# mLSTM heads of a hybrid layer: a head's first values and keys begun in the third chunk of the head in front, its second pair's in its own first chunk

## The chip, the cores and the metric

The kernel runs on one core of one Trainium2 chip. The metric is device time in microseconds (us) of one execution. An execution has a span, from the first to the last instruction that the profile shows, and a little time around it. Before the change three timed runs gave 1699.35, 1700.01 and 1708.68 us, median 1700.01.

## The reference, cut to what matters

One decoder layer over 2048 tokens of width 1024, batch 1, all in float32. An RMS norm, one input projection, two groups of heads beside each other, one output projection, a residual and a last norm:

```
u = rms_norm(x, norm_g)
q_g, k_g, v_g, z_g, r_g, x_m, z_m = split(u @ w_in)
o_g = gla(q_g, k_g, v_g, log_sigmoid(r_g @ up + b) / 16)       # 4 heads, key 128, value 256
c   = silu(causal_conv4(x_m) + conv_b)                          # 1024 wide
q_m, k_m, v_m = c @ blockdiag(w_q), c @ blockdiag(w_k), x_m @ blockdiag(w_v)
i, f = gates of [q_m, k_m, v_m]
h_m = mlstm(q_m, k_m, v_m, i, f)                                # 4 heads of 256
o_m = (rms_norm(h_m) * g + skip * c) * silu(z_m)
out = rms_norm(x + [rms_norm(o_g) * g * silu(z_g), o_m] @ w_out)
```

The mLSTM part is a recurrence per head with a matrix state C and a vector state n: C = f C + i v kT, n = f n + i k, and h = C q / max(|n q|, 1), with exponential input gates and a running maximum that keeps them in range. It may be done chunk by chunk: inside a chunk by a masked 'attention' matrix, between chunks by the state. Only this part of the kernel is touched.

## The kernel before, in words

**Stages.** The tokens are cut into 4 blocks of 512, a block into 4 chunks of 128. TensorE (PE) goes through the input projections of the mLSTM group for the 4 blocks, then through those of the GLA group for the 4 blocks, then through the output projection. A float32 product of full accuracy is made of three fp32r matmuls on a high and a low part (`mm3`, line 193; three matmuls with 512 columns are one *step* of the projection below). One projected tile of 128 x 512 is 8 steps (24 matmuls, tile `pp`); a block of the mLSTM group has 16 of them: X0 to X7 (`xm_drain`, the first two taken as a pair, 16 steps) and Z0 to Z7 (`zm_drain`, the last two as a pair).

**The heads.** Between the steps of the projection PE does the heads, `mattn(b, h)` from line 810. A head forms `pqp` (queries, line 818), then `pma` (line 831, the chunk-by-chunk attention matrices), which `asplit` (line 784) takes out of PSUM: a copy on ScalarE (ACT) and a subtraction on VectorE (DVE), then a mask on GpSimd (POOL). `prep_v(p)` (line 842) forms the values of chunk pair p: 4 matmuls into `pmv`, two copies on ACT and two fused operations on DVE that make `v1` and `v1l`, and two small DVE copies. `prep_c(p)` (line 860) forms the keys: 4 transposes into `pmc`, one copy on ACT (`ctk`, line 869), one subtraction on DVE (`ctl`, line 870). `prep_q(c)` (line 875) splits the queries of chunk c into `qx` with one copy on ACT and one subtraction on POOL; it does nothing for chunk 0 of block 0. None of the three starts a DMA or uses SyncE.

Then come the 4 chunks (line 891). A chunk needs `C`, a scaled copy of the state in two parts (lines 898 and 899, two buffers, so both are in use until the chunk before is through with them); `pmu` (line 904), the state's update, 6 matmuls that read `v1` and `ctk`, `ctl`; `pmo` (line 912), the output, 3 matmuls on the attention matrix and 6 on `qx` and `C`; and the norm of the output (lines 918 to 931: `dn`, `r`, `jk`, `rs`, `on`). Chunks 0 and 1 read pair 0, chunks 2 and 3 pair 1. At the end `fin_pair` (line 795, twice) transposes the outputs (`pt`) and multiplies in the gains and the gate; `spill` sends them to memory. `v1`, `v1l`, `ctk`, `ctl` have two buffers each, one a pair. All of `pqp`, `pma`, `pmv`, `pmc` and `pt` share the two PSUM slots of the pool `ps_t`.

**What sets the order.** PE's order is written out by hand, by a planner: class `Order`, line 104. Projection and heads are generators. The planner keeps a clock `od.t` that each planned matmul advances by a nominal length; a generator that yields a number is due again that much later, one that yields a name waits until the name is in `od.done`. Of those due, the oldest head goes first, then the younger one, then the projection (line 129); the projection yields after every step. Two heads are active at a time (line 126): the third is begun when the first is done. The two PSUM slots are planned for by `od.wait()` and `od.hold(drain)`: after a use, the slot counts as free `drain` us of planned time later; after `pma` that is `od.hold(0.00)` (line 833). The other engines' order is found by a scheduler from priorities; `ahead(tc, n)` and `at(tc, n)` move instructions n places forward. Each engine then works its list off in that order, and real waits are semaphores.

**Around the change.** A head that has its attention matrix waits for the name `mm` of the head in front (line 881), set when that head's chunk 3 is issued (line 942). Then it does

```
        yield from od.wait()
        prep_q(0)
        prep_v(0)
        od.hold(1.80)
        yield from od.wait()
        prep_c(0)
        od.hold(1.10)
        yield 2.10
```

and its chunks. Behind chunk 0 it issues `prep_v(1)`, behind chunk 1 `prep_c(1)` (line 938), each with `od.hold(2.10)`, and between chunks it yields 0.20 and 1.90.

Of the kernel before, what the change touches and what calls it, by code (L numbers as in the profile page):

```python
# [25 lines left out]
H = 4  # L26
# [60 lines left out]
@contextmanager  # L87
def ahead(tc, n):

    tc.cur_priority -= n  # L90
    yield
    tc.cur_priority += n


def at(tc, n):
    def wrap(f):
        def g(*a):
            with ahead(tc, n):
                return f(*a)
        return g  # L100
    return wrap
# [58 lines left out]
def fast_path(ctx, tc, inside, xT, x, w_fm, w_v, w_r, wqT, wkT, wvT, wv, wg, w_up, b_g,  # L160
              norm_g, gla_g, conv_w, conv_b, b_if, ml_g, skip, w_out, fin_g, out):
    nc = tc.nc
    od = Order(tc)
# [24 lines left out]
    def mm(o, l, r, start, stop, **k):  # L188
        n = o.free_size()
        od.t += max(n, 256) / 2400.0 if l.dtype == F32R else max(4 * n, 64) / 2400.0  # L190
        nc.tensor.matmul(o, l, r, start=start, stop=stop, **k)  # L191
# [618 lines left out]
    def mattn(b, h):  # L810
        yield f"x{b}"
        yield 4.00
        qp = gq.tile([P, 2, TB], F32, name="qp", tag="qp", bufs=3)
        ost = gp.tile([P, 2, TB], F32, name="ost", bufs=2)
        for e in range(2):
            t = 2 * h + e
            yield from od.wait()
            pq = ps_t.tile([P, TB], F32, name="pqp", tag="pt")
            mm(pq, wqk[:, t, :], cm[t], True, True)
            with ahead(tc, HPP):  # L820
                nc.scalar.copy(qp[:, e, :], pq)
            with ahead(tc, HPO):
                nc.scalar.activation(ost[:, e, :], cm[t], AF.Copy, scale=skp[:, t:t + 1])
            od.hold(2.40)
            yield 0
        yield from od.wait()
        pa = ps_t.tile([P, TB], F32, name="pma", tag="pt")
        for c in range(NC):
            cs = slice(c * P, (c + 1) * P)
            for e in range(2):  # L830
                mm(pa[:, cs], cm[2 * h + e][:, cs], qp[:, e, cs], e == 0, e == 1)
        A = asplit(pa)
        od.hold(0.00)
        yield f"gr{b}"
        wk, wkh, wkl, ga, fl = gts[b]
        if h not in Tm:
            Tm[h] = gp.tile([P, 2, 258], F32, name=f"Tm{h}", tag=f"T{h}")
        T = Tm[h]
        kv = {}

        @at(tc, HPV)
        def prep_v(p):
            pv = ps_t.tile([P, 2, 2, P], F32, name="pmv", tag="pt")
            v1 = gp.tile([P, 2, 258], F32R, name="v1", tag="v1", bufs=2)
            v1l = gp.tile([P, 2, 258], F32R, name="v1l", tag="v1l", bufs=2)
            for i in range(2):
                c = 2 * p + i
                for e in range(2):
                    mm(pv[:, i, e, :], xm[2 * h + e][0][:, 4 + c * P:4 + (c + 1) * P], wvs[:, 2 * h + e, :], True, True)
            for i in range(2):  # L850
                w1 = wk[:, 2 * p + i, h:h + 1]
                p1 = pv[:, i].rearrange("p e t -> p (e t)")
                nc.scalar.activation(v1[:, i, 0:DV], p1, AF.Copy, scale=w1)
                nc.vector.scalar_tensor_tensor(v1l[:, i, 0:DV], p1, w1, v1[:, i, 0:DV].bitcast(F32), op0=ALU.mult, op1=ALU.subtract)
                kv[2 * p + i] = [(v1[:, i, :], v1l[:, i, :]), None]
            for x_, w_ in ((v1, wkh), (v1l, wkl)):
                nc.vector.tensor_copy(x_[:, :, DV:DV + 2], w_[:, 2 * p:2 * p + 2, h:h + 1].bitcast(F32).broadcast_to([P, 2, 2]))

        @at(tc, HPV)
        def prep_c(p):  # L860
            pv = ps_t.tile([P, 2, 2, P], F32, name="pmc", tag="pt")
            ctk = gp.tile([P, 2, 2, P], F32R, name="ctk", tag="ctk", bufs=2)
            ctl = gp.tile([P, 2, 2, P], F32R, name="ctl", tag="ctl", bufs=2)
            for i in range(2):
                c = 2 * p + i
                for e in range(2):
                    tr(pv[:, i, e, :], cm[2 * h + e][:, c * P:(c + 1) * P])
                kv[c][1] = (ctk[:, i], ctl[:, i])
            nc.scalar.copy(ctk, pv)
            nc.vector.tensor_tensor(ctl, pv, ctk.bitcast(F32), op=ALU.subtract)  # L870

        qx = {}

        @at(tc, HPQ)
        def prep_q(c):
            if c < NC and (b or c):
                qx[c] = gp.tile([P, 2, 2, P], F32R, name="qx", tag="ca", bufs=2)
                split(qx[c][:, 0], qx[c][:, 1], qp[:, :, c * P:(c + 1) * P], QX)

        if (b, h) != (0, 0):  # L880
            yield f"mm{b}_{h - 1}" if h else f"mm{b - 1}_{H - 1}"
        yield from od.wait()
        prep_q(0)
        prep_v(0)
        od.hold(1.80)
        yield from od.wait()
        prep_c(0)
        od.hold(1.10)
        yield 2.10
        on = {}  # L890
        for c in range(NC):
            cs = slice(c * P, (c + 1) * P)
            first = b == 0 and c == 0
            last = b == NB - 1 and c == NC - 1
            if not first:
                Ch, Cl = (gp.tile([P, 2, 258], F32R, name="C", tag="C", bufs=2) for i in range(2))
                with ahead(tc, HPX):
                    nc.scalar.activation(Ch, T, AF.Copy, scale=ga[:, c, h:h + 1])
                    nc.vector.scalar_tensor_tensor(Cl, T, ga[:, c, h:h + 1], Ch.bitcast(F32), op0=ALU.mult, op1=ALU.subtract)
            v1, ctk = kv[c]  # L900
            if not last:
                for e in range(2):
                    pu = ps_u.tile([P, 258], F32, name="pmu", tag="pu")
                    mm3(pu, (ctk[0][:, e, :], ctk[1][:, e, :]), v1, True, True)
                    with ahead(tc, HPT):
                        if first:
                            nc.scalar.copy(T[:, e, :], pu)
                        else:
                            nc.vector.scalar_tensor_tensor(T[:, e, :], T[:, e, :], ga[:, c, h:h + 1], pu, op0=ALU.mult, op1=ALU.add)
                yield 0  # L910
            po = ps_o.tile([P, 258], F32, name="pmo", tag="po")
            mm3(po, (A[:, c, :], A[:, NC + c, :]), v1, True, first)
            if not first:
                for e in range(2):
                    mm3(po, (qx[c][:, 0, e, :], qx[c][:, 1, e, :]), (Ch[:, e, :], Cl[:, e, :]), False, e == 1)
            prep_q(c + 1)
            with ahead(tc, HPN):
                r = sp.tile([P, 1], F32, name="r", bufs=4)
                dn = sp.tile([P, 1], F32, name="dn")
                nc.vector.tensor_scalar(dn, po[:, DV:DV + 1], -1.0, fl[:, c, h:h + 1], op0=ALU.mult, op1=ALU.max)  # L920
                nc.vector.tensor_tensor(r, dn, po[:, DV:DV + 1], op=ALU.max)
                nc.vector.reciprocal(r, r)
                jk = sp.tile([P, DV], BF16, name="jk", bufs=1)
                ss = sp.tile([P, 1], F32, name="ss", bufs=4)
                nc.scalar.activation(jk, po[:, 0:DV], AF.Square, scale=r, accum_out=ss)
                rs = sp.tile([P, 1], F32, name="rs", bufs=4)
                rsqrt(rs, ss, DV)
                nc.vector.tensor_tensor(rs, rs, r, op=ALU.mult)
                o = gp.tile([P, DV], F32, name="on", bufs=4)
                if MON:  # L930
                    nc.scalar.activation(o, po[:, 0:DV], AF.Copy, scale=rs)
                else:
                    nc.vector.tensor_scalar(o, po[:, 0:DV], rs, None, op0=ALU.mult)
            on[c] = o
            yield 0.20
            if c < 2:
                yield from od.wait()
                (prep_v, prep_c)[c](1)
                od.hold(2.10)
            if c < NC - 1:  # L940
                yield 1.90
        od.done.add(f"mm{b}_{h}")
        if f"z{b}_{h}" not in od.done:
            yield f"z{b}_{h}"
        yield from od.wait()
        fin_pair([on[0], on[1]], zsm[b, h], mlg[:, 2 * h:2 * h + 2], 0, ost, True)
        od.hold(1.80)
        yield 3.50
        yield from od.wait()
        fin_pair([on[2], on[3]], zsm[b, h], mlg[:, 2 * h:2 * h + 2], 2 * P, ost, True)  # L950
        od.hold(2.80)
        spill(b, KT + 2 * h, ost)
        od.done.add(f"m{b}_{h}")
# [823 lines left out]
```

## Time and profile before

| | before |
|---|---|
| timed runs (us) | 1699.35, 1700.01, 1708.68; median 1700.01 |
| the profiled execution (us) | 1708.55 |
| its span (us) | 1706.3 |
| PE busy in the span | 1621.9 us (95%) |
| DVE, ACT, POOL busy | 56%, 41%, 26% |
| mean granted TensorE clock | 0.982 of full speed |
| stage: mLSTM heads | about 111 to 702 us |

The busy time of PE is the sum of its matmuls as the profile models them, so 95% says that PE is hardly ever without a matmul in flight; what is left is idle time, and a view of the waits names what ended each piece of it. A line of the timeline gives the start, the length, the engine, the line of the kernel, the operation, output <- inputs, the shapes and the count of the merged instructions; in square brackets the idle time of that engine just before and what ended it. Matmuls overlap, so their length is more than their share of the time; the distance of two starts is what one costs. The granted clock is 1.00 at 2.4 GHz and 0.50 at 1.2 GHz; a stretch's figure is the mean.

### The profile page before, as it was taken

Reading aid. Unit: us, or ns where it says so; the run is one execution under the profiler, and the core shown is the slowest. Engines: PE = TensorE matmul, PEld = TensorE weight load, DVE = VectorE, ACT = ScalarE, POOL = GpSimd, SP = SyncE. Lnnn points to the kernel's source line nnn. Section 1 sums busy time; section 2 is a strip of 40 time slices with the busy share of each in tenths; the row PEclk is TensorE's granted clock in tenths of the full one; section 3 lists DMA queues with packets and bytes.
Section 4 is the critical chain, followed back from the end, with each engine's and each line's share of the span. In section 5 each row is a group of like instructions: output and inputs, shape, how many; then the busy total and the mean of one; then the engine's idle time right before and its main releaser. Section 6 shows DMA issues by size and latency. Waiting matters only on the chain.

```text
span 1706.3 us, 25559 instructions
## 1 busy us (share of the span) xinstructions
PE 1621.9 (95%) x8840; PEld 1362.2 (80%) x8840; DVE 954.7 (56%) x2125; ACT 695.3 (41%) x1486; POOL 444.4 (26%) x422
## 2 busy tenths in 40 slices
PE   7989899999999999899999999999999999999997
PEld 5768777887888788789888888888888877887776
DVE  4956775775667577734442334233513556567663
ACT  4656754564455455412232223122313433243331
POOL 3433421220121024344303120302031304223330
PEclk9999999999999999999999999999999999999999
DMA  7577667636564766576858685758575565574441
GB/s 269 198 261 240 227 218 233 193 111 212 196 196 149 228 195 201 195 251 218 311 168 305 201 283 190 253 173 285 193 252 199 168 237 200 166 247 136 162 145 67
DMA packets 221258, 355.42 MB, mean 208 GB/s; under 512 B 24368, under 2 KB 58160, under 8 KB 221120
## 3 DMA queue, kind: packets, MB, share of 16 engines
q1 hardware_dynamic: 221120, 353.70, 62.5%
q8 instruction: 72, 1.18, 0.3%
q14 instruction: 66, 0.54, 0.1%
HBM read 253.86 MB, written 102.89 MB: 209 GB/s over the span
## 4 chain that ended last, share of the span: by engine, by line
PE 45%; DMA 5%; DVE 4%; issue 2%; POOL 2%; ACT 2%; SPq 0%; POOLq 0%; DVEq 0%; ACTq 0%
PE py L191 16%; PE pp L191 15%; PE pv L191 9%; PE po L191 2%; DMA wlo<-w_dr 1%; DMA whi<-w_dr 1%; DVE bc L1078 1%; PE pu L191 1%; POOL ring L1213 1%; PE pt L201 1%; PE pa L191 1%; DMA f<-q_dr 1%; DMA ring<-in_w_out 0%; PE ptk L201 0%; DMA o1l<-o_dr 0%
## 5 line engine op out<-in xcount | busy, mean ns | idle before, releaser
L191 PE MATMUL pp<-uh,whi 128*128 128x512 f32 x1008 | 421.5, 418 | 11.9 <-ACT whi L214 6.0
L191 PE MATMUL pp<-ul,whi 128*128 128x512 f32 x1008 | 400.1, 397 | 0.5 <-DVE ul L404 0.4
L191 PE MATMUL pp<-uh,wlo 128*128 128x512 f32 x1008 | 400.3, 397 | 0.0
L191 PEld LDWEIGHTS pp<-uh,whi 128*128 128x128 f32 x1008 | 192.0, 190 | 52.6 <-ACT whi L214 7.1
L191 PEld LDWEIGHTS pp<-uh,wlo 128*128 128x128 f32 x1008 | 191.4, 190 | 47.4 <-DMA wlo<-w_dr 1.1
L191 PEld LDWEIGHTS pp<-ul,whi 128*128 128x128 f32 x1008 | 192.0, 190 | 39.9 <-issue 4.8
L215 POOL TENSOR_TENSOR wlo<-wraw,whi 128x512 fp32r<-128x512 f32 (+1 forms) x97 | 133.5, 1382 | 159.2 <-ACT whi L214 56.7
L1213 POOL TENSOR_TENSOR ring<-ring,ring 128x512 f32<-128x512 f32 x77 | 106.1, 1383 | 247.0 <-DMA ring<-in_w_out 117.2
L191 PE MATMUL pv<-whi,uh 128*128 128x256 f32 (+1 forms) x512 | 151.5, 296 | 15.5 <-DVE zs L581 8.8
L191 PE MATMUL pv<-wlo,uh 128*128 128x256 f32 (+1 forms) x512 | 148.5, 290 | 0.5 <-DMA wlo<-w_dr 0.5
L191 PE MATMUL pv<-whi,ul 128*128 128x256 f32 (+1 forms) x512 | 148.4, 290 | 0.0
L191 PE MATMUL py<-f,as 128*128 128x512 f32 x540 | 135.0, 402 | 9.4 <-DVE yf L1308 4.2
L214 ACT CAST as<-ring 128x512 fp32r<-128x512 f32 x105 | 65.0, 621 | 169.3 <-PE py L191 118.1
L191 PEld LDWEIGHTS py<-f,as 128*128 128x128 f32 x540 | 103.6, 193 | 35.2 <-ACT f L214 9.3
L215 POOL TENSOR_TENSOR qx<-qp,qx 128x256 fp32r<-128x256 f32 x60 | 55.7, 932 | 274.8 <-ACT qx L214 274.8
L191 PEld LDWEIGHTS pv<-whi,uh 128*128 128x128 f32 x512 | 100.1, 196 | 18.0 <-DVE zs L581 9.6
L191 PEld LDWEIGHTS pv<-wlo,uh 128*128 128x128 f32 x512 | 99.9, 195 | 1.6 <-DMA wlo<-w_dr 1.6
L191 PEld LDWEIGHTS pv<-whi,ul 128*128 128x128 f32 x512 | 100.1, 195 | 0.7
L215 DVE TENSOR_TENSOR as<-ring,as 128x512 fp32r<-128x512 f32 x105 | 84.8, 811 | 12.2 <-ACT as L214 11.4
L645 DVE SCALAR_TENSOR_TENSOR c<-xm,cw,c 128x512 f32<-128x512 f32 x96 | 78.2, 822 | 14.2 <-ACT c L643 13.4
L221 POOL TENSOR_TENSOR grs<-rsa,nhalf 128x2 f32<-128x2 f32 x32 | 23.6, 738 | 198.4 <-DVE rsa L220 187.7
L985 DVE TENSOR_TENSOR vl<-pv,v 128x256 fp32r<-128x256 f32 x56 | 23.5, 422 | 89.3 <-ACT v L983 89.3
(341 smaller groups left out, 3156.5 us busy)
## 6 DMA issues: line engine op xcount, KB each, us to landing
whi<-w_dr SPq DMA_DIRECT2D x212, 256.0 KB, 3.8
wlo<-w_dr SPq DMA_DIRECT2D x212, 256.0 KB, 4.2
wraw<-in_w_fm SPq DMA_DIRECT2D x80, 256.0 KB, 3.9
w_dr<-whi SPq DMA_DIRECT2D x76, 256.0 KB, 3.4
w_dr<-wlo SPq DMA_DIRECT2D x76, 256.0 KB, 3.4
o_dr<-ost SPq DMA_DIRECT2D x64, 256.0 KB, 3.5
ring<-o_dr SPq DMA_DIRECT2D x60, 256.0 KB, 3.1
ul<-u_dr SPq DMA_DIRECT2D x56, 256.0 KB, 4.6
```

Source lines behind the costliest of these rows:

```text
L191: nc.tensor.matmul(o, l, r, start=start, stop=stop, **k)
L201: nc.tensor.transpose(o, i, ident)
L214: nc.scalar.copy(hi, raw)
L215: (nc.gpsimd if "l" in pool else nc.vector).tensor_tensor(lo, raw, hi.bitcast(F32), op=ALU.subtract)
L221: nc.gpsimd.tensor_tensor(dst, a, nhalf.broadcast_to(list(src.shape)), op=ALU.pow)
L645: nc.vector.scalar_tensor_tensor(ca, xt[:, 1 + j:1 + j + TB], cw[:, t, j:j + 1], ca, op0=ALU.mult, op1=ALU.add)
L985: nc.vector.tensor_tensor(vl[b, h][t // 2][:, t % 2, :], pv[:, :DV], vv[b, h][:, t, :].bitcast(F32), op=ALU.subtract)
L1078: nc.vector.tensor_tensor_scan(w3[:, c], ones, w3[:, c], 0.0, op0=ALU.mult, op1=ALU.add)
L1213: nc.gpsimd.tensor_tensor(o, a, b, op=ALU.subtract)
```

## The change

The wait on the head in front is cut in two. The new name `mp` is set in chunk 2 of a head, after its 0.20. The next head waits for it, and then does `prep_v(0)`, `prep_c(0)` and its 2.10; only then it waits for `mm`, if that isn't set yet, and does `prep_q(0)`, which stood ahead of `prep_v(0)`. The second pair's two preparations both stand behind chunk 0, each with its own wait and hold, and nothing behind chunk 1.

```diff
+        before = f"{b}_{h - 1}" if h else f"{b - 1}_{H - 1}"
         if (b, h) != (0, 0):
-            yield f"mm{b}_{h - 1}" if h else f"mm{b - 1}_{H - 1}"
+            yield "mp" + before
         yield from od.wait()
-        prep_q(0)
         prep_v(0)
         od.hold(1.80)
         yield from od.wait()
         prep_c(0)
         od.hold(1.10)
         yield 2.10
+        if (b, h) != (0, 0) and "mm" + before not in od.done:
+            yield "mm" + before
+        prep_q(0)
         on = {}
         for c in range(NC):
...
             yield 0.20
-            if c < 2:
-                yield from od.wait()
-                (prep_v, prep_c)[c](1)
-                od.hold(2.10)
+            if c == 0:
+                for prep in (prep_v, prep_c):
+                    yield from od.wait()
+                    prep(1)
+                    od.hold(2.10)
+                    yield 0
+            if c == 2:
+                od.done.add(f"mp{b}_{h}")
             if c < NC - 1:
                 yield 1.90
```

## Rows read from the trace of the kernel before

**Rows 1.** The page's first part: busy time of each engine, share of the span, instructions.

```profile
PE 1621.9 (95%) x8840; PEld 1362.2 (80%) x8840; DVE 954.7 (56%) x2125; ACT 695.3 (41%) x1486; POOL 444.4 (26%) x422
```

**Rows 2.** PE's waits between 100 and 700 us: who waited for whom; us in total, times, longest.

```profile
PE pmu L191 <- DVE ctl L870: 9.7, 14, 1.2
PE pmu L191 <- ACT ctk L869: 8.8, 7, 2.9
PE pt L201 <- DVE v1l L854: 4.5, 4, 1.8
```

**Rows 3.** The timeline at chunk 2 of head 0 of block 0: PE's `pmc` of the second pair, ACT's work, and PE's next `pmu`.

```profile
123.03 0.60 PE L201 MATMUL pmc<-ident,c 128*128 128x128 f32 x4
...
127.55 0.47 ACT L925 ACTIVATE jk<-pmo,r 128x256 bf16<-128x256 f32 x1 [1.00 <-DVE r L922]
...
128.01 0.58 ACT L869 CAST ctk<-pmc 128x512 fp32r<-128x512 f32 x1
...
128.64 0.58 PE L191 MATMUL pmu<-v,ctk 128*128 128x258 f32 x1 [2.92 <-ACT ctk L869]
...
129.78 0.58 PE L191 MATMUL pmu<-v,ctl 128*128 128x258 f32 x1 [0.35 <-DVE ctl L870]
```

**Rows 4.** Four stretches of the span: stretch, length, busy time of PE, PEld, DVE, ACT, POOL with their instructions, mean granted clock, DMA share, GB/s. Below them starts of the projection's matmuls at either level of the clock.

```profile
126.00:136.00 10.00, 7.02 (x25) 6.05 (x26) 7.07 (x19) 4.83 (x13) 4.46 (x6) 0.66 0.77 262
208.00:218.00 10.00, 6.83 (x30) 5.28 (x29) 9.32 (x29) 7.86 (x17) 4.17 (x5) 0.83 0.46 152
290.00:300.00 10.00, 7.89 (x46) 6.49 (x45) 7.59 (x24) 6.14 (x16) 2.69 (x4) 1.00 0.51 161
453.00:461.00 8.00, 6.12 (x26) 5.23 (x26) 4.80 (x17) 3.63 (x10) 1.97 (x3) 0.79 0.41 132
...
133.59 0.63 PE L191 MATMUL pp<-uh,wlo 128*128 128x512 f32 x1
134.02 0.63 PE L191 MATMUL pp<-uh,whi 128*128 128x512 f32 x1
...
135.14 0.40 PE L191 MATMUL pp<-uh,whi 128*128 128x512 f32 x1
135.37 0.40 PE L191 MATMUL pp<-ul,whi 128*128 128x512 f32 x1
```

**Rows 5.** PE's timeline from the end of head 1 to chunk 0 of head 2 in block 1, and the first `pqp` of head 3.

```profile
327.21 0.88 PE L191 MATMUL pmo<-C,qx 128*128 128x258 f32 x6
327.93 0.39 PE L191 MATMUL pp<-uh,whi 128*128 128x512 f32 x1
...
328.62 0.60 PE L201 MATMUL pt<-ident,on 128*128 128x128 f32 x4
329.06 1.06 PE L191 MATMUL pmv<-wvs,xm 128*128 128x128 f32 x8
329.87 0.48 PE L191 MATMUL pp<-uh,whi 128*128 128x512 f32 x1
...
331.35 0.60 PE L201 MATMUL pmc<-ident,c 128*128 128x128 f32 x4
...
333.18 0.60 PE L201 MATMUL pt<-ident,on 128*128 128x128 f32 x4
...
334.32 0.28 PE L191 MATMUL pmu<-v,ctk 128*128 128x258 f32 x1
...
336.82 1.06 PE L191 MATMUL pmv<-wvs,xm 128*128 128x128 f32 x8
...
338.40 1.02 PE L191 MATMUL pqp<-c,wqk 128*128 128x512 f32 x2
```

**Rows 6.** How `pma`'s slot is drained: PE, ACT and DVE behind chunk 2 of head 2 in block 0, and ACT and DVE where no chunk stands ahead (block 1, before the heads).

```profile
184.18 1.95 PE L191 MATMUL pma<-qp,c 128*128 128x128 f32 x16
185.89 0.48 PE L191 MATMUL pp<-uh,whi 128*128 128x512 f32 x1
...
187.10 0.48 ACT L931 ACTIVATE on<-pmo,rs 128x256 f32<-128x256 f32 x1 [1.36 <-DVE rs L928]
187.47 0.58 ACT L788 CAST A<-pma 128x512 fp32r<-128x512 f32 x1
...
188.09 0.69 DVE L789 TENSOR_TENSOR A<-pma,A 128x512 fp32r<-128x512 f32 x1 [1.02 <-ACT A L788]
...
268.66 0.59 ACT L788 CAST A<-pma 128x512 fp32r<-128x512 f32 x1 [2.44 <-PE pma L191]
...
269.34 0.68 DVE L789 TENSOR_TENSOR A<-pma,A 128x512 fp32r<-128x512 f32 x1
```

**Rows 7.** ACT, DVE and POOL right behind chunk 3 of head 1 in block 1: `C` and `qx` of head 2's chunk 0.

```profile
328.01 0.73 ACT L898 ACTIVATE C<-Tm,ga 128x516 fp32r<-128x516 f32 x1 [1.87 <-PE pmo L191]
328.65 0.39 ACT L214 CAST qx<-qp 128x256 fp32r<-128x256 f32 x1
...
328.78 0.76 DVE L899 SCALAR_TENSOR_TENSOR C<-Tm,ga,C 128x516 fp32r<-128x516 f32 x1
...
329.12 1.00 POOL L215 TENSOR_TENSOR qx<-qp,qx 128x256 fp32r<-128x256 f32 x1 [1.07 <-ACT qx L214]
```

**Rows 8.** How `pmv`'s slot is drained: a second pair's `pmv` and its last DVE operation (block 1, head 1).

```profile
312.12 1.05 PE L191 MATMUL pmv<-wvs,xm 128*128 128x128 f32 x8
...
315.71 0.48 DVE L854 SCALAR_TENSOR_TENSOR v1l<-pmv,wk,v 128x256 fp32r<-128x256 f32 x1 [0.93 <-ACT v L853]
```

## The prediction, made before the change was built

> **What bounds the kernel now.** Read the page's first part first: PE has a matmul in flight for 1621.9 us, 95% of the span, while DVE has 56% and ACT 41% [rows 1]. The change adds no work to any engine. It can only take idle time from PE, give it new idle time, or change the clock at which PE works. So the next view is PE's waits in the heads' stage [rows 2]: 9.7 + 8.8 = 18.5 us in 21 waits of `pmu` for `ctl` and `ctk`, and 4.5 us in 4 waits of a `pt` for the slot of a `pmv`. All 21 lie at a chunk 2, the first reader of the second pair. The timeline at the worst shows why [rows 3]: `pmc` was issued at 123.03, but its copy stands in ACT's list behind `jk`, which waited for the norm's `r`; `ctk` began at 128.01, and PE stood still for 2.92 us, then 0.35 more for `ctl`. Last, the clock behind such waits [rows 4]: behind three of them it is granted at half (1.2 GHz) for a while. A mean of 0.66 over 10 us is 6.8 us at half, 0.83 over 10 us is 3.4, 0.79 over 8 us is 3.4: 13.6 us. At half a projection matmul costs 134.02 - 133.59 = 0.43 us, at full 0.23, so 13.6 x (1 - 0.23/0.43) = 6.3 us are lost there. (The fourth stretch holds such waits too, PE idle for 2.1 us of 10, and stayed at 1.00.)
>
> The Trainium skill (TensorE: Matmul & The Clock Gate, section Terms) prices throttled time at that time x (1 - K/N); at half this makes 13.6 x 0.5 = 6.8 us, an estimate; the trace has 6.3, and the sum takes the trace's.
>
> **The change part by part.** Times are those of the profiled execution, 1708.55 us (span 1706.3 and 2.25 around it), which is 8.5 us above the median of 1700.01; the difference worked out on the one is carried to the other.
>
> *(a) The second pair's keys, a chunk earlier.* Now `pmc` has three steps of the projection, chunk 1 and four steps between itself and chunk 2: 3 x 0.70 + 1.8 + 4 x 0.70 = 6.7 us (a step is 3 x 0.23; in a chunk 6 matmuls take 327.93 - 327.21 = 0.72 [rows 5], 0.12 each, and it has 15). The slowest case of before took from the end of `pmc` (123.63) to the second wait's end (129.78) 6.1 us [rows 3]. So the 21 waits go: -18.5, and with them the three stretches at half clock: -6.3. If the cover were too short, each us missing would come back at its chunk 2. What is late next is the slots of PSUM, (c) and (d).
>
> *(b) `prep_q(0)` behind the wait.* It is passed by `prep_v(0)` and `prep_c(0)`: its ACT copy stands behind three more ACT copies, its POOL subtraction behind none. Chunk 0 now may follow chunk 3 of the head in front at once, with one step, `pt`, `pmu` and 3 matmuls of `pmo` between: 0.70 + 0.44 (329.06 - 328.62) + 0.72 + 0.36, less the 0.16 by which the next matmul begins before the modelled end: some 2.1 us from the end of the last `pmo`. What is needed just there can be seen [rows 5, 7]: that `pmo` ends at 327.21 + 0.88 = 328.09; `C` begins on ACT at 328.01 and is whole on DVE at 329.54, `qx` on POOL at 330.12, 1.45 and 2.03 us after. Both just fit, because the scheduler puts early what is ready early. Bounds: nothing gained, since no wait for `qx` is in the trace; lost at most the 1.4 us of a `qx` from start to end (328.65 to 330.12), at 6 places (two heads in each of blocks 1 to 3): 0 to 8 us. I take 0, the row that is at that very place.
>
> *(c) The first pair, begun at `mp`.* Here the order must be followed through the planner, whose nominal lengths fix only the order (a step 0.64, a chunk 1.61, `prep_v` 0.85, `prep_c` 0.43, `fin_pair` 0.43, `pqp` 0.85, `pma` 1.71). I did this by hand; for the kernel before it gives exactly the sequence of rows 5. Put 0 at a block's first `prep_v(0)`. Head 0 does chunk 0 at 3.8, then `prep_v(1)` and `prep_c(1)`, chunk 1 at 9.3, chunk 2 at 13.5, `mp` at 15.7. Head 1, ready since before the heads, prepares its first pair 15.7 to 17.0; chunk 3 of head 0 at 17.6, its first `fin_pair` at 19.9, chunk 0 of head 1 at 20.3, 1.1 us behind that chunk in place of the 334.32 - 328.09 = 6.2 us of rows 5. But head 2 is begun only when head 0 is done (25.8), pays its 4.00, and has `pqp` at 32.0 and 32.8. Then chunk 3 of head 1 (35.0), `pma` of head 2 (36.6), `fin_pair` of head 1 (38.3) and `prep_v(0)` of head 2 (38.7) follow each other without a step between. Head 3, begun at 43.0, has chunk 2 of head 2 (53.7), its `pma` (55.3), its `prep_v(0)` (57.0) and `prep_c(0)` (57.8), again without a step. So twice in each block a preparation needs the slot that `pma` holds, and the planner lets it, for `od.hold(0.00)` says that slot is free at once. Before, chunk 3 and three steps stood there.
>
> What the slot takes: `pma` ends at 186.13, ACT's copy begins at 187.47 behind `on`, DVE is through at 188.78, 2.65 us after the end; where no chunk stands ahead, 268.66 + 1.36 [rows 6]. The next matmul may begin 0.24 before that end (185.89). Head 2: `pt` takes 0.44, `prep_v(0)` waits 2.65 + 0.24 - 0.44 = 2.4 us. Head 3: `prep_v(0)` takes 0.81 (329.06 to 329.87 [rows 5]), `prep_c(0)` waits 2.1 us. All of PE's list waits behind it, the chunks and the projection too. 4 blocks x 4.5 = +18 us. With the short drain it is 4 x (1.15 + 0.85) = 8 us. I take 18, since a chunk with its `on` stands ahead both times, as in the long row; the ends stay 8 and 18.
>
> These would be even gaps that recur at one place of every block. The Trainium skill (Perfetto Trace Analysis, section Optimization Strategy) says that consistent bubbles can mean that PSUM has no room for the next tile; it has no price for it, and the gaps of before aren't of this kind, as they wait for `ctk` and `ctl` to be written.
>
> *(d) The last `fin_pair` behind `prep_v(1)`.* For heads 0 and 2 its `pt` now takes the slot of the next head's second `pmv`, with `pmc` and three steps between: 0.44 (as `pt`, 4 transposes) + 3 x 0.70 - 0.24 = 2.3 us after its end. A second pair's `pmv` ended at 313.17 and was drained at 316.19, 3.0 us after [rows 8]: 0.7 us of wait, 8 times, +5.6. In exchange the 4 waits of rows 2 go, -4.5: together +1.1. Bounds: -4.5 if nothing waits, and 8 x 1.8 - 4.5 = +9.9 if each is as long as the longest of rows 2.
>
> *(e) The clock behind the new waits.* Of the waits of before, the 2.92 us was followed by 6.8 us at half, others by 3.4 us, and those of the fourth stretch by none [rows 3, 4]. I let three of the eight of (c) have 3.4 us at half, 3.4 x 0.465 = 1.6 each: +4.7. Bounds 0 and 8 x 3.2 = 25 (6.8 us each).
>
> Sum: -18.5 - 6.3 + 0 + 18 + 1.1 + 4.7 = -1.0 us: 1707.5 for the profiled execution, 1699 against the median. The GLA and output stages keep their work and, but for a small shift at their start, their order: 0.
>
> **The rivals.** *All gain:* the slots are free in time. ACT's order is made anew, and if `A`'s copy no longer stands behind `on`, the drain is 1.36 us: -18.5 - 6.3 + 8 and (d) at 0, no clock lost: -17, 1683 us. For it: no wait for `pma`'s slot is among rows 2, and 1.36 us has occurred [rows 6]. Against: the same two instructions would stand there in the same distance.
>
> *Slower:* one mechanism, the eight waits of (c) take the clock with them. Its place is each `pmv` or `pmc` right behind a `pma`. The other terms make -23.7, so it breaks even at 3.0 us a place and is over 0.5% slower from (23.7 + 8.5)/8 = 4.0. A wait of 2.25 with 3.4 us at half makes 3.85; with half of them at 6.8 us 4.65, or +37 in all: +13.5, 1713 us. For it: three of the waits of before did so. Against: the fourth stretch of rows 4, as much idle, didn't.
>
> *It doesn't do what it says:* my planner's walk is wrong and a third wait for the name `mp` or a drain brings the preparations back to where they were; then (a) is given back in part and nothing else changes: about -5 to 0, 1697.
>
> **How the numbers follow.** Within 0.5% (8.5 us, about what a measurement of this kernel can tell from no change) lie the forecast and the third rival. Forecast 0.43, all gain 0.31, slower 0.21, the third 0.05. A small part of the forecast's own range (1690 to 1708) is beyond 0.5%: faster 0.33, same 0.45, slower 0.22. The range goes from the all-gain case to the slower one: 1682 to 1713.
>
> **What would show it.** (a) is right if no `pmu` waits for `ctk` or `ctl` any more. (c) is right if PE's waits list `pmv` and `pmc` for DVE `A` of line 789, four each, of 2.4 and 2.1 us; wrong, if they are under 1 us or the two names don't occur. (b) is wrong if `pmo` waits for `qx` or `C`. (d) shows as `pt` waiting for `v1l`, eight times instead of four. (e) shows in the granted clock behind the waits of (c). Behind chunk 3 of heads 0 and 2 the next head's chunk 0 should begin after some 1.1 us, behind that of head 1 as late as now or later. The prediction falls with (c): without those waits the kernel is 1% faster.

## The result, and the profile after

The changed kernel takes 1722.9 us (median of 4 runs), the kernel before 1701.7 (median of 4, three of them those of the table above): the ratio is 1.012, 95% interval 1.0101 to 1.014. Forecast were 1699 us, range 1682 to 1713: it is slower, and outside the range. The profiled execution after is 1721.2 us with a span of 1719.4; that of before lay 7 us above its own median, so the two profiles differ by 12.7 us only. For the heads' stage there is a better mark in the same two traces: the first `pa`, with which the heads of the GLA group begin, starts at 747.1 us before and at 765.6 after, 18.5 later. Its row in each:

```profile
747.14 0.38 PE L191 MATMUL pa<-qt,kt 128*128 128x128 f32 x2
...
765.60 0.38 PE L191 MATMUL pa<-qt,kt 128*128 128x128 f32 x2
```

The page's first part shows the same work as [rows 1]:

```profile
PE 1625.9 (95%) x8840; PEld 1367.8 (80%) x8840; DVE 958.7 (56%) x2125; ACT 693.4 (40%) x1486; POOL 439.7 (26%) x422
```

PE's waits of the changed kernel from 100 to 710 us (us in total, times, longest); they answer to [rows 2]. The lines of a chunk have numbers 3 higher than before, those behind `mattn` 7 higher.

```profile
PE pmv L191 <- DVE A L789: 12.4, 4, 4.0
PE pmc L201 <- DVE A L789: 11.1, 4, 3.7
PE pt L201 <- DVE ctl L870: 7.2, 10, 1.0
PE pt L201 <- ACT on L934: 3.1, 1, 3.1
PE pmu L191 <- DVE Tm L912: 1.4, 4, 0.6
PE pt L201 <- DVE v1l L854: 1.3, 1, 1.3
...
PE pmu L191 <- DVE ctl L870: 0.8, 1, 0.8
```

Only two of these rows wait for data that they read, `pt` for `on` and `pmu` for `ctl`. `pmv` doesn't read `A`, `pmc` doesn't read `A`, `pt` doesn't read `ctl`: each waits for a slot of PSUM whose last reader is the instruction named, and so do `pmu` for `Tm` and `pt` for `v1l`. That is how a slot wait looks in this view. The 18.5 us for `ctk` and `ctl` have gone down to 0.8; 23.5 us for the slot that `pma` held have come, and `pt` waits 11.6 in place of 4.5.

The timeline of block 3, from `pma` of head 2 to the `pmv` behind it (the counterpart of [rows 6]):

```profile
650.13 1.95 PE L191 MATMUL pma<-qp,c 128*128 128x128 f32 x16
...
651.50 1.77 POOL L215 TENSOR_TENSOR wlo<-wraw,whi 128x512 fp32r<-128x512 f32 x1
...
652.15 0.15 DVE L220 TENSOR_SCALAR rsa<-ss 128x1 f32<-128x1 f32 x1
653.24 0.72 POOL L215 TENSOR_TENSOR qx<-qp,qx 128x256 fp32r<-128x256 f32 x1
...
653.92 0.54 POOL L221 TENSOR_TENSOR rs<-rsa,nhalf 128x1 f32<-128x1 f32 x1
...
654.50 0.16 DVE L931 TENSOR_TENSOR rs<-rs,r 128x1 f32<-128x1 f32 x1 [2.19 <-POOL rs L221]
...
654.69 0.47 ACT L934 ACTIVATE on<-pmo,rs 128x256 f32<-128x256 f32 x1 [2.57 <-DVE rs L931]
655.06 0.58 ACT L788 CAST A<-pma 128x512 fp32r<-128x512 f32 x1
655.67 0.69 DVE L789 TENSOR_TENSOR A<-pma,A 128x512 fp32r<-128x512 f32 x1 [0.62 <-ACT A L788]
...
656.51 0.68 PE L191 MATMUL pmv<-wvs,xm 128*128 128x128 f32 x4 [3.99 <-DVE A L789]
```

Read it from the bottom. PE stood still for 3.99 us ahead of `pmv`. The slot came free with DVE's subtraction; that had ACT's copy of `A` ahead of it, which stood behind `on`; `on` waited for `rs`, and `rs` for POOL, for which `rsa` was ready at 652.30, but which did a piece of the projection's weights (`wlo`) and a `qx` first. So a drain of two instructions, 0.58 + 0.69 = 1.3 us, lasted 4.3 us from the end of `pma` (652.08) to that of `A` (656.36).

In the table, for each kernel's profile: PE's waits from 100 to 710 us added up over the view's rows, the parts of them that matter, and the time at half clock in that stretch, added up from the trace's clock records. Each ratio is to the kernel before, timed beside it. The stretch is the same time in all, not the same work: in kernels 7, 10 and 11 it takes in a wait of 2.8 us of the GLA group (`pv` for `zs`) that ends behind 710 us in the others.

| kernel | ratio to before | all waits | `pmv`, `pmc` for `A` | `pmu` for `ctk`, `ctl` | `pt` | half clock |
|---|---|---|---|---|---|---|
| before | 1 | 26.4 | 0 | 18.5 | 4.5 | 13.7 |
| changed | 1.012 | 39.9 | 23.5 | 0.8 | 11.6 | 27.3 |
| 1: changed, hold 2.40 | 0.9963 | 25.1 | 0.7 | 1.9 | 10.0 | 17.1 |
| 2: second pair's half alone | 0.9951 | 20.9 | 0 | 0.3 | 7.2 | 13.7 |
| 3: first pair's half alone | 1.0036 | 30.6 | 0 | 13.9 | 6.6 | 10.2 |
| 4: before, hold 2.40 | 1.0006 | 31.3 | 0 | 19.1 | 8.1 | 13.7 |
| 5: changed, norm later | one run | 47.1 | 23.3 | 0.6 | 20.1 | 44.4 |
| 6: changed, queries first | 1.011 | 40.2 | 22.4 | 1.9 | 11.9 | 13.7 |
| 7: as 2, hold 2.80 | 0.9916 | 22.4 | 0 | 0 | 4.9 | 13.7 |
| 8: as 1, holds 3.10 | 0.9962 | 24.2 | 1.2 | 0.3 | 7.4 | 10.2 |
| 9: changed, no power | one run | 20.1 | 14.4 | 0 | 1.6 | 13.8 |
| 10: before, no power | 0.9912 | 18.8 | 0 | 11.1 | 1.3 | 6.8 |
| 11: as 9, timed | 0.9915 | 24.4 | 16.8 | 0.8 | 1.7 | 6.8 |

### The profile page after: what moved, and what is told of

Read it like the earlier page. It is cut to its first block, busy times and chain, and to the rows that moved or that the text cites. A ratio compares the mean times of both kernels' runs of the same rounds, so it can differ in the third digit from the quotient of the medians.

```text
span 1719.4 us, 25574 instructions
## 1 busy us (share of the span) xinstructions
PE 1625.9 (95%) x8840; PEld 1367.8 (80%) x8840; DVE 958.7 (56%) x2125; ACT 693.4 (40%) x1486; POOL 439.7 (26%) x422
## 4 chain that ended last, share of the span: by engine, by line
PE 70%; DVE 11%; DMA 6%; issue 4%; POOL 4%; ACT 4%; SPq 1%; POOLq 0%; ACTq 0%; DVEq 0%
PE pp L191 32%; PE py L191 14%; PE pv L191 10%; PE po L191 2%; PE pmo L191 2%; PE pqp L191 1%; PE pmu L191 1%; POOL rs L221 1%; PE pt L201 1%; DVE bc L1085 1%; DVE C L902 1%; PE pu L191 1%; POOL wlo L215 1%; PE pma L191 1%; DMA whi<-w_dr 1%
## 5 line engine op out<-in xcount | busy, mean ns | idle before, releaser
L191 PE MATMUL pv<-whi,uh 128*128 128x256 f32 (+1 forms) x512 | 150.7, 294 | 13.8 <-DVE zs L581 8.8
L215 DVE TENSOR_TENSOR as<-ring,as 128x512 fp32r<-128x512 f32 x105 | 85.1, 813 | 12.4 <-ACT as L214 11.6
L221 POOL TENSOR_TENSOR grs<-rsa,nhalf 128x2 f32<-128x2 f32 x32 | 23.3, 729 | 197.7 <-DVE rsa L220 187.0
```

What stands on the lines that cost most here:

```text
L215: (nc.gpsimd if "l" in pool else nc.vector).tensor_tensor(lo, raw, hi.bitcast(F32), op=ALU.subtract)
L221: nc.gpsimd.tensor_tensor(dst, a, nhalf.broadcast_to(list(src.shape)), op=ALU.pow)
```

## The experiments

**1. The slot that `pma` holds, planned for.** In the changed kernel:

```diff
         A = asplit(pa)
-        od.hold(0.00)
+        od.hold(2.40)
```

> The changed kernel with one figure altered: the planner counts pma's slot as free 2.40 us later in place of 0.00. Theory (the slots): the eight waits of pmv and pmc for DVE A of line 789, 23.5 us in the changed kernel, fall under 4 us, with them most of the 13.7 us of additional half clock in the heads' stage; the chunk 2 waits stay away. Time 1690 to 1698, ratio to before 0.993 to 0.998. Rival (the tighter heads overload ACT and DVE, the slot is only where it shows): the idle time turns up at other names, pt, pmu, pmo, and the time stays over 1715.

Measured: 1695.8 us, ratio 0.9963 (0.9947 to 0.998), 27 us less than the changed kernel's 1722.9 and 6 less than the kernel before beside it. PE's waits then read

```profile
PE pt L201 <- DVE ctl L870: 9.4, 10, 2.0
PE pmo L191 <- DVE C L902: 3.9, 5, 1.5
...
PE pmv L191 <- DVE A L789: 0.7, 2, 0.5
```

One number that only fixes PE's order takes 23.5 us of waits for `A` down to 0.7, and 10.2 us of half clock with them. So the loss comes from the slots, as the planner places their users, and not from the change's idea; in block 1, four steps of the projection (324.77 to 327.63 us in this trace) now stand between the `pma` and the `pmv` of head 2.

**2. The second pair's keys alone.** In the kernel before:

```diff
-            if c < 2:
-                yield from od.wait()
-                (prep_v, prep_c)[c](1)
-                od.hold(2.10)
+            if c == 0:
+                for prep in (prep_v, prep_c):
+                    yield from od.wait()
+                    prep(1)
+                    od.hold(2.10)
+                    yield 0
```

> The kernel before with only the second pair's keys moved behind chunk 0; the first pair waits for mm as before. Theory: prep_v(0) and prep_c(0) stand where they stood, chunk 3 and steps of the projection lie between pma and them, so no wait for A; the 18.5 us of pmu at chunk 2 go and half clock with them: 1680 to 1690, ratio 0.987 to 0.994. Rival (the waits of pt for the second pair's ctl come from the two preparations standing together behind chunk 0): pt waits 7 us or more here too and the ratio is 0.994 to 1.000.

Measured: 1693.2 us, ratio 0.9951 (0.9936 to 0.9966): faster, but by 8 to 9 us where 12 to 22 were expected: a miss, with a ratio in the rival's range. The waits:

```profile
PE pt L201 <- DVE v1l L854: 7.2, 6, 2.0
PE pmo L191 <- DVE C L899: 3.4, 5, 1.8
PE pmu L191 <- DVE Tm L909: 3.0, 3, 2.0
PE pmc L201 <- DVE ost L805: 2.9, 2, 1.6
```

The 18.5 us for `ctk` and `ctl` are gone, as in the whole change; about two thirds come back at what is late next, the slots and the state. The rival's 7 us of `pt` are there too, but for the slot of `pmv` (`v1l`), not for that of `pmc` (`ctl`). The half clock stayed at 13.7 us, at other places. The ratio overlaps that of experiment 1, so the first pair begun at `mp` has no gain that shows, even with its slot planned for.

**3. The first pair begun at `mp`, alone.** In the changed kernel the second pair's preparations are put back as they were (the diff above, reversed).

> The changed kernel with the second pair's keys back behind chunk 1. Theory: the slot waits of pmv and pmc stay (about 20 us), and the waits of pmu for ctk and ctl at chunk 2 are back (about 18 us): slower than the changed kernel by 10 to 20 us, 1733 to 1743, ratio 1.018 to 1.025. Rival (the loss comes from the second pair's move): no slower than before, ratio 1.000 to 1.005.

Measured: 1707.2 us, ratio 1.0036 (1.0019 to 1.0053): a miss. The number lies in the rival's range, but its reason, a loss by the second pair's move, doesn't hold, for that move alone is faster (experiment 2). No `pmv` or `pmc` waits for `A` here. Block 1 shows why; PE's timeline from `pma` of head 2:

```profile
317.19 1.83 PE L191 MATMUL pma<-qp,c 128*128 128x128 f32 x14 [0.78 <-ACT qp L821]
318.77 0.48 PE L191 MATMUL pp<-uh,whi 128*128 128x512 f32 x1
...
320.65 0.89 PE L191 MATMUL pmo<-C,qx 128*128 128x258 f32 x6
321.37 0.83 PE L191 MATMUL pmv<-wvs,xm 128*128 128x128 f32 x6
```

A step and a whole chunk stand between `pma` and `pmv`: from the end of the one (319.02) to the start of the other there are 2.35 us of work, and nothing waits. With `prep_c(1)` behind chunk 1 again, the second `pqp`, and `pma` right behind it, come at another place against the chunks. So -0.5% and +0.4% don't add up to the +1.2% of both: the collision of (c) needs both halves. What this half has by itself: 13.9 us for `ctk` and `ctl` are left, `pma` waits 7.0 us for `qp`, and `pt` 6.6.

**4. The hold alone.** The edit of experiment 1, in the kernel before.

> The kernel before with the planner counting pma's slot as free 2.40 us later. Theory: chunk 3 and steps of the projection stood behind pma anyway, so the order behind it stays and only the four pqp at the start of a block move: ratio 0.998 to 1.002. Rival: the hold by itself is worth time, and e1 would owe it its gain: ratio under 0.996.

Measured: 1701.2 us, ratio 1.0006 (0.9989 to 1.0022), as expected. The hold has no gain of its own; it mends what the change broke.

**5. The norm placed later.** In the changed kernel:

```diff
-HPN = 60
+HPN = -60
```

> The changed kernel with the norm's instructions (the chain from dn to on) 120 places further back in the scheduler's priorities; PE's order is the same. In ACT's list A's copy then stands ahead of the last on at three of the eight places at which pmv or pmc follows pma (second place of block 0, as in the changed kernel, and now the first places of blocks 1 and 2); at the other five it stands behind on, as before. If the drain of pma's slot is long because A's copy stands behind on, which waits for the norm's rs: the pmv waits for A of blocks 1 and 2 fall from 2.36 and 2.35 us to 1.4 to 1.9, and the five others stay at 2.3 us or more. Rival, the wait is the length of the drain itself wherever A stands (2.3 us or more in blocks 1 and 2 as well, unless the clock differs). In the total both make little: 1715 to 1728.

Measured (one run): 1739.0 us, and the waits of blocks 1 and 2 did not fall to 1.4 to 1.9, they rose to 3.26 and 2.98. A miss, and the most telling one. Block 1:

```profile
329.67 0.59 ACT L788 CAST A<-pma 128x512 fp32r<-128x512 f32 x1
...
330.54 0.55 POOL L221 TENSOR_TENSOR rs<-rsa,nhalf 128x1 f32<-128x1 f32 x1
331.12 0.16 DVE L931 TENSOR_TENSOR rs<-rs,r 128x1 f32<-128x1 f32 x1 [1.24 <-POOL rs L221]
331.20 0.48 DVE L805 SCALAR_TENSOR_TENSOR ost<-pt,mlg,ost 128x256 f32<-128x256 f32 x1
...
331.60 0.68 DVE L789 TENSOR_TENSOR A<-pma,A 128x512 fp32r<-128x512 f32 x1
...
332.43 0.98 PE L191 MATMUL pmv<-wvs,xm 128*128 128x128 f32 x3 [3.26 <-DVE A L789]
```

ACT's copy does stand ahead of `on` here and is through at 330.26. But DVE's subtraction, the slot's last reader, stands behind `rs`, and that waits for POOL. So "behind `on` in ACT's list" was half of the mechanism: the chunk's norm stands ahead of `A` in DVE's list too, and the norm goes through POOL. The theory was changed to that. (The 16 us over the changed kernel come from elsewhere: `pt` waits 11.5 us for the late `on` in place of 3.1, and 44.4 us are at half clock in place of 27.3.)

**6. The queries first again.** In the changed kernel `prep_q(0)` is put back ahead of `prep_v(0)`:

```diff
         yield from od.wait()
+        prep_q(0)
         prep_v(0)
...
             yield "mm" + before
-        prep_q(0)
```

> The changed kernel with prep_q(0) back ahead of prep_v(0), and so ahead of the second wait on the head in front; PE's order is the same. Step (b) of the prediction puts this move at 0: then the ratio to the kernel before stays at 1.009 to 1.015 (1717 to 1728), A's eight waits at 20 to 27 us. Rival, late queries and what they push back on ACT and POOL cost something (bound 8 us): 1711 to 1716, with the small waits for C, Tm and r (some 3 us) gone.

Measured: 1718.7 us, ratio 1.011 (1.0092 to 1.0127), which overlaps that of the changed kernel. Step (b) holds: the move costs nothing that can be measured. PE's order is the same here, and `A`'s waits nearly so; what differs is the clock.

**7. The second pair's half with its slots planned for.** To experiment 2 is added:

```diff
         prep_v(0)
-        od.hold(1.80)
+        od.hold(2.80)
```

> The kernel before with only the second pair's keys moved behind chunk 0, and with the hold behind prep_v(0) 2.80 in place of 1.80. Theory: the 7.2 us in 6 waits of pt for v1l that were left over come from the planner's counting that slot free too soon; they fall under 2.5 us and the time to 1686 to 1691 (ratio 0.991 to 0.995). Rival, the waits only move to another user of the slots or to the chunks: 1691 to 1697, the sum of PE's waits in the heads' stage as before it.

Measured: 1686.9 us, ratio 0.9916 (0.9896 to 0.9936), the best of all, and in the range of the theory. But the waits say less:

```profile
PE pt L201 <- DVE v1l L854: 4.9, 7, 2.0
PE pmc L201 <- DVE ost L805: 4.5, 3, 2.7
```

4.9 us are more than the 2.5 expected, and others took their place. The sum of 22.4 holds the 2.8 us of `pv`, a wait that ends behind 710 us in experiment 2 (the row below); without them it is 19.6 against 20.9.

```profile
PE pv L191 <- DVE zs L581: 2.8, 1, 2.8
```

Where the last 6 us came from, this view of one execution doesn't show, and the two intervals meet at 0.9936; it stays open.

**8. All holds longer.** To experiment 1 is added `od.hold(3.10)` in place of `od.hold(2.10)` behind `prep(1)`.

> The changed kernel with 2.40 behind pma (as in the first experiment) and 3.10 in place of 2.10 behind the second pair's two preparations. Theory: the 9.4 us in 10 waits of pt for ctl are the same fault of the planner's numbers; they fall under 4 us and the time to 1687 to 1692 (ratio 0.991 to 0.995). Rival, the drains are as long as the work in front of them allows and the waits only move: 1693 to 1699.

Measured: 1694.2 us, ratio 0.9962 (0.9949 to 0.9975), the same as without. `pt` waits 5.3 us for `ctl` instead of 9.4, where under 4 were expected, and the sum stays (24.2 against 25.1): the time is the rival's, these waits only move.

**9. The changed kernel without the norm's power on POOL.** This kernel leaves out the root in `rs`; all else is computed.

```diff
-                rsqrt(rs, ss, DV)
+                nc.vector.tensor_scalar(rs, ss, DV * EPS, None, op0=ALU.add)
```

> The changed kernel with the norm's power on POOL left out (rs is the sum of squares with its small constant, times r, without the root; everything else is computed). PE's order is the same, and in DVE's list rs still stands ahead of A's subtraction at all eight places. Theory, formed from the run with the norm placed later: the slot of pma is held until the norm of the chunk in front is through POOL, because rs, which waits for POOL, stands ahead of A on DVE. In the changed kernel rs on DVE begins 1.17, 0.66, 0.98, 0.66, 0.98, 0.67, 2.20 and 0.98 us after the end of rsa (8.3 in all); these go, so A's eight waits fall from 23.5 to 13 to 17 us, the longest, the 3.99 of block 3, to about 1.8. Rival, the slot is held by ACT's list or by the copies themselves: the waits stay at 20 us or more. Time, by the theory 1706 to 1716, by the rival 1716 to 1727.

Measured (one run): 1696.9 us. PE's order is unchanged, and

```profile
PE pmv L191 <- DVE A L789: 7.9, 4, 2.7
PE pmc L201 <- DVE A L789: 6.5, 4, 2.0
```

make 14.4 us, 9.1 less than 23.5, where the eight gaps between `rsa` and `rs` added up to 8.3; the 3.99 of block 3 is 1.85. The second theory holds for the slots, though only for a part of their time: 14.4 us stay without POOL's step. The time fell by more than it said (1706 to 1716), since the `pt` waits went as well, from 11.6 to 1.6 us, and the half clock from 27.3 to 13.8.

**10 and 11. The control.** The same edit in the kernel before, and experiment 9 again beside it, timed.

> The kernel before with the norm's power on POOL left out, PE's order the same: the control for the run of the changed kernel without it (1696.9). If the power costs the changed kernel through the slots of PSUM, the kernel before, whose waits are for ctl, ctk and one v1l, has less to gain: the waits for ctl and ctk stay at 10 to 19 us, time 1688 to 1700 (0 to 12 us less), and what the change adds falls from +21 to between 0 and +10. Rival, the power slows both alike, by POOL's and DVE's load: the kernel before falls by the same 20 to 25 us, to 1675 to 1681.

> The changed kernel without the norm's power once more, timed in the same session as the kernel before without it: 1694 to 1704, A's eight waits 13 to 17 us; by the rival of that run (POOL's load alone) about 1.2% above the kernel before without the power.

Measured: 1687.0 us (ratio 0.9912, 0.9882 to 0.9941) without the change, 1688.2 (0.9915, 0.9889 to 0.9941) with it. The control fell by 15 us, a little more than the 0 to 12 expected and less than the rival's 20 to 25, so POOL's step costs every version something. But the difference that the change makes is 1 us without it, 21 with it. Experiment 11 came out below its 1694 to 1704 as well. `A`'s waits remain at 16.8 us in it and take the place of 11.1 for `ctk` and `ctl` in the control. The control's rows:

```profile
PE pmu L191 <- ACT ctk L869: 7.0, 7, 2.0
PE pmu L191 <- DVE ctl L870: 4.1, 15, 1.0
```

Those of experiment 11:

```profile
PE pmc L201 <- DVE A L789: 9.0, 4, 2.6
PE pmv L191 <- DVE A L789: 7.8, 4, 2.7
```

## Why the prediction was wrong

The terms of its sum, and what the profiles have for them. Half clock is priced as in the prediction, at 0.465 of its time.

| term | forecast (us) | measured (us) |
|---|---|---|
| (a) waits for `ctk` and `ctl` | -18.5 | 0.8 - 18.5 = -17.7 |
| (a) the clock behind them | -6.3 | 13.7 x 0.465 = -6.4 |
| (b) `prep_q(0)` | 0 | 0, experiment 6 |
| (c) the slot of `pma` | +18 | +23.5 |
| (d) `pt` | +1.1 | 11.6 - 4.5 = +7.1 |
| (e) the clock behind the new waits | +4.7 | 27.3 x 0.465 = +12.7 |
| other waits | 0 | 4.0 - 3.4 = +0.6 |
| sum | -1.0 | +19.8 |

The sum measured agrees with the 18.5 us at the GLA heads' start and the 21.2 of the medians. Nearly all of the error lies in three terms, all of them too small: (c) by 5.5 us, (d) by 6.0 and (e) by 8.0.

*(a) was right*, to 0.8 us. *(b)* stays at 0: no `pmo` waits for `qx`, and those for `C` are 0.8 us in 2 waits, 0.9 in 3 before.

*(c) was right in its mechanism and short in its size.* The planner's walk gave four `pmv` and four `pmc`, at head 2 and head 3 of each block, and that is what waits. In blocks 1 and 2 chunk 0 of the next head begins 0.9 us behind chunk 3 of head 2 and 9.9 behind that of head 1 (6.2 before), as the walk had it; behind that of head 0 it is 2.2 to 2.3 and not 1.1, with waits of `pt` in it. At head 2 of blocks 1 and 2 the size is right too: a drain of 2.65 us and waits of 2.36 and 2.35, against 2.4. The other two there are 3.66 and 3.99, and those of head 3 are 1.72, 2.56, 3.67 and 3.20 against 2.1; the drains of these six last 2.56 to 4.51 us. The step that failed is the drain of 2.65 us, carried over from the row of before as if it were a length [rows 6]. More rows would not have warned: in the kernel before it is 2.65 or 2.66 us at all eight of these places. But it is a queue: `on` in that row already waited for `rs`, and how long `rs` takes depends on what POOL has ahead of it. Experiments 5 and 9 show it, the first by failing. POOL is not the whole of the queue: without its step 14.4 to 16.8 of the 23.5 us stay (experiments 9 and 11). In the longest drain (4.51 us, with the wait of 3.67) DVE stood only 0.66 us for POOL; there a `th`, a `C`, a `qx` and `jk` were ahead of `on` and `A` on ACT, and a `zs` and a `C` ahead of the norm's `rs` on DVE.

*(d) was mis-sized by 6.0 us, and named the wrong slot.* The sum let eight `pt` wait for the slot of a `pmv`; only one does, ten wait for that of a `pmc` (`ctl`), and one waits 3.10 for `on`. They are not only the last `fin_pair` of heads 0 and 2: the first one waits too (0.72 us behind chunk 3 of head 0 in block 1), since the next head's `prep_c(0)` now stands just ahead of that chunk. Its bound of +9.9 held.

*(e) was mis-sized by 8.0 us, the largest error.* 10.2 us at half were allowed for, 27.3 came in this execution. 20.5 of them lie at four of the waits of (c), 6.8 behind two `pt` waits, to which the prediction gave no clock at all.

*The rivals.* The one called slower is what happened: by its price, (23.5 + 20.5 x 0.465) / 8 = 4.1 us a place, over its 4.0 and below the 4.65 with which it made 1713. What it lacked is (d), 6.0 us and another 3.2 of clock. All gain fell with (c): `A`'s copy stands behind `on` in seven places of eight. (By its own rows its short drain makes 1.36 + 0.24 - 0.81 = 0.79 us at head 3, not 0.85; 7.8 us in all in place of 8.) The third rival is out: the change does what it says.

The chances followed from one choice, 2.65 us as the likely drain with a shorter one as its only alternative in (c). A longer drain had no case of its own, although `jk`'s wait for `r` [rows 3] and `on`'s for `rs` [rows 6] showed that lists stand still there for 1.00 and 1.36 us.

## What to carry to other kernels

Work begun early gains only if the buffers that it uses are free by then; where a plan says that a slot is free at once, look up what stood between two of its users before, and what will stand there after. A drain's length read from a row is the length of a queue, and a new order makes a new queue: list what is ahead of it on every engine that reads the buffer, and on the engines that those wait for. The Trainium skill (Perfetto Trace Analysis, section Optimization Strategy) says that consistent bubbles can mean PSUM without room for the next tile; the eight waits of 23.5 us agree in that a slot of PSUM is what lacked, though they weren't even (1.72 to 3.99 us) and went with another order and no more room. The row that tells them is a matmul waiting for an instruction whose output it doesn't read.

## What was not expected of the hardware

The same waits don't always take the clock. The changed kernel and that of experiment 6 have one order on PE and nearly the same waits. Take `pmc` of head 3 in blocks 2 and 3, in the changed kernel; first its rows in the timeline, then the two stretches around it (columns as in [rows 4]).

```profile
515.61 1.11 PE L201 MATMUL pmc<-ident,c 128*128 128x128 f32 x4 [3.67 <-DVE A L789]
...
682.09 1.12 PE L201 MATMUL pmc<-ident,c 128*128 128x128 f32 x4 [3.20 <-DVE A L789]
```

```profile
512.00:522.00 10.00, 6.39 (x28) 5.93 (x29) 5.38 (x15) 3.87 (x10) 2.06 (x3) 0.66 0.03 11
...
680.00:690.00 10.00, 7.91 (x38) 7.23 (x39) 5.14 (x16) 3.99 (x10) 2.78 (x4) 0.66 0.23 89
```

The same two views of the kernel of experiment 6:

```profile
515.30 0.66 PE L201 MATMUL pmc<-ident,c 128*128 128x128 f32 x4 [2.92 <-DVE A L789]
...
679.38 0.66 PE L201 MATMUL pmc<-ident,c 128*128 128x128 f32 x4 [3.18 <-DVE A L789]
```

```profile
513.00:523.00 10.00, 7.70 (x57) 7.25 (x58) 7.45 (x23) 5.24 (x12) 3.16 (x5) 1.00 0.03 10
...
677.00:687.00 10.00, 7.62 (x55) 7.15 (x56) 7.31 (x23) 5.51 (x13) 3.90 (x5) 1.00 0.26 98
```

A wait of 3.20 us went with a mean of 0.66 of full speed around it, one of 3.18 at the same place with 1.00; over the stage, 27.3 us at half against 13.7. `pmc` itself takes 1.1 us in the one and 0.66 in the other. So what the clock adds to a wait could be bounded from the traces, but not forecast for a single one; the ratios of the two kernels, each over several executions, differ by 0.001. Nor is one profile the clock of its kernel: over whole executions the mean was 0.977 to 0.983 in the four of the changed kernel and 0.979 to 0.988 in the five of experiment 6.
